# Two more seven-product pairs in three branch blocks, sums by accumulating transfers, and four plain pairs in front of the first

## The chip, the cores and the metric

The kernel runs on one core of a Trainium2 chip. The metric is the time of one execution in microseconds of the device, lower is better. The time before is the median of three runs, 1035.17 us (1033.79 to 1035.41).

The engines named below: TensorE (PE in the profile, its weight loads PEld) multiplies; VectorE (DVE), ScalarE (ACT) and GpSimd (POOL) work on tensors; SyncE (SP) issues the weight loads from memory. Each engine takes its instructions from one queue, in order.

## The reference

One decoder layer on 256 tokens of width 2048, with two branches that are merged and projected once more:

```python
h = _rmsnorm(x, pre_norm_g)
proj = einsum('bsd,de->bse', h, w_in)      # q_a, c_kv, k_rope, z_mla, c_in, ..., g_mla, g_conv
...                                        # latent attention; a gated short convolution
y_mla  = einsum('bse,ed->bsd', attn, w_o_mla)
y_conv = einsum('bse,ed->bsd', b_gate * conv * silu(z_conv), w_o_conv)
merged = sigmoid(g_mla) * y_mla + sigmoid(g_conv) * y_conv
out = einsum('bsd,de->bse', merged, w_out)
return x + _rmsnorm(out, post_norm_g)
```

Everything is float32. The change touches four products of 256 x 2048 by 2048 x 2048: `g_mla` and `g_conv` (columns of `w_in`), `y_mla` and `y_conv`.

## The kernel before

*Weights.* They are streamed in units of 1 MB, in the order of a list `plan`, in which a unit's number is its place. SyncE loads a unit into a `raw` tile (three of them); ScalarE rounds it into a high part `whi`, VectorE subtracts to get a low part `wlo` (`split_act`, line 282 and 283). Both are in halves of 128x1024 (`whi122_0`, `whi122_1024`), five slots each: a half can be written when the half five places before it was read for the last time. A product is three matmuls, high by high, high by low, low by high (`product`), each 128x128 by 128x512.

*Blocks.* The four products at issue are cut in eight blocks (n, c): n = 0 and 1 are the two gates, n = 2 and 3 the two branches (`y_mla`, `y_conv`), c is the half of the columns, 1024 wide. A block has eight pairs, one unit each, so block (0,0) has the units 113 to 120, (0,1) 121 to 128, and so on to (3,1), 169 to 176. A *plain pair* has 8 products of 2x2 quarters (two row tiles of x, two column halves, two inner halves), 24 matmuls. A *seven-product pair* is the same 2x2 product by Strassen's way in Winograd's form: 7 products, 21 matmuls. It needs sums of weight quarters, which VectorE makes (`ts`, `split_seven`, line 224) and which are split in high and low too (`th`, `tl`, two slots each), and sums of activation quarters (`mixed`, lines 1008 and 1012, split into `mix0`, `mix3`, `mix5`, kept for later blocks). Which pairs have seven products is in `fast`: pairs 0, 3 and 5 (`FAST`) in the gates' blocks, but 0 and 3 in (0,0); none in the branches' blocks.

*A fast block* (`fast_block`) accumulates its products in eight PSUM banks, p1, q5, q7, q6, p2, q3, q4, d22. Plain pairs go to p2, q3, q4 and d22 alone. Behind the last seven-product pair p1, q5, q6 and q7 are complete, and `first_sums` adds them up (one copy on ScalarE, line 1053, and four sums on VectorE, line 1050); it is put in the program at the start of the pair after the last fast one. `last_sums` adds p2, q3, q4 and d22 behind the block's end, again on VectorE. The bank of p1, that of q5 and so on are the same ones in the next block, whose pair 0 begins with p1, q5, q7, q6. Then ScalarE makes the sigmoid of the gates (line 1115).

*A plain block* (`plain_block`) accumulates in four banks. Behind it VectorE multiplies the sums by the gates (lines 1131, 1137), and in the blocks of n = 3 adds the branches.

*The order of the work.* TensorE's matmuls are kept in program order; the instructions of the other engines are put in order by a scheduler, within what their data allow, so each engine's queue is fixed before the run. `pair_order` sets the order of pairs, and so of units. Between pairs, `between(i)` puts other work into the program: the mixed activations and the turning of the attention's and convolution's results.

Of the kernel before, what the change touches and what calls it, by code (L numbers as in the profile page):

```python
# [84 lines left out]
def tile_layer(ctx: ExitStack, tc: tile.TileContext, xw, w0, xb, x, pos, pvec, post_g, wc, wz, wcv, wkr, wqk, wqr, wv, cwr, wd, wo, out):  # L85
# [53 lines left out]
            u_head[i][j] = add(wcv[i, j])  # L139

    pair_order = {(n, c): list(range(PAIRS)) for n in range(4) for c in range(2)}
    pair_order[0, 0] = [1, 2, 4, 0, 6, 3, 5, 7]
    fast = {(n, c): FAST if n < 2 else () for n in range(4) for c in range(2)}
    fast[0, 0] = FAST[:2]
    u_d, seven = {}, set()
    for n in range(4):
        for c in range(2):
# [148 lines left out]
    def col(name, k=0):  # L296
        o, _ = PV[name]
        return pv[:, o + k : o + k + 1]

    const.tile([P, P], F32, name="place")  # L300
    mhalf = const.tile([P, 1], F32, name="mhalf")
    nc.gpsimd.memset(mhalf[:, :], -0.5)
    hpi = const.tile([P, 1], F32, name="hpi")
# [4 lines left out]
    one = nc.const_aps.tensor(1.0, [P, P], F32)  # L308
    for _ in range(8):
        matmul(idle[:, :P], one, one, start=True, stop=True)  # L310
    const.tile([P, LINE - 8 + 112 + P], F32, name="const_pad")
    cos_t = const.tile([P, S], F32, name="cos_t")
    sin_t = const.tile([P, S], F32, name="sin_t")
    r_x = const.tile([P, S], F32, name="r_x")
    r_both = const.tile([P, LINE], F32, name="r_both")
    nc.gpsimd.memset(r_both[:, :], 0.0)
    r_col, r_sq = r_both[:, :NT], r_both[:, NT : 2 * NT]
# [92 lines left out]
    def input_norm():  # L410
        ss = squares("x", [(x_tok[:, t, :], x_tok[:, t, :]) for t in range(NT)])
        v = temp("v_x", (P, NT), tag="rms_v")
        nc.vector.tensor_scalar(v[:, :], ss[:, :], 1.0 / D, EPS, op0=ALU.mult, op1=ALU.add)
        inverse_root(r_col[:, :], v[:, :])
        nc.vector.tensor_tensor(r_sq[:, :], r_col[:, :], r_col[:, :], op=ALU.mult)

        rt = temp("r_turned", (P, LINE), bufs=1)
        temp("pad_n", (P, S - LINE), bufs=1)
        nc.vector.transpose(rt[:, :], r_both[:, :])
        far = dram.tile([NT, S // NT], F32, name="far_r")  # L420
        rows_of = rt[:, :].rearrange("(q y) x -> y q x", q=4)
        for t in range(NT):
            tc.keep_in_program_order(
                nc.gpsimd.dma_start(out=far[t, :].rearrange("(q x) -> q x", q=4), in_=rows_of[t])
            )
        return lambda: tc.keep_in_program_order(
            nc.gpsimd.dma_start(out=r_x[:, :], in_=far[:, :].rearrange("t s -> (t s)").unsqueeze(0).to_broadcast([P, S]))
        )


# [4 lines left out]
        nc.vector.tensor_tensor(dst, ps[:, :S], t[:, :], op=ALU.add)  # L435

    def rows(dst):
        tc.keep_in_program_order(nc.vector.tensor_tensor(dst, dst, r_x[:, :], op=ALU.mult))


    tables_pi = temp("ta_i", (P, SQ), I32, 1)
# [1 line left out]
    def tables():  # L443
# [38 lines left out]
        for o in range(4):  # L482
# [3 lines left out]
                    tc.keep_in_program_order(nc.gpsimd.tensor_copy(dst[to, SQ * q : SQ * (q + 1)], src[ti, :]))  # L486
        yield
        tc.keep_in_program_order(
            nc.vector.tensor_scalar(sin_t[:, :], sin_t[:, :], col("sign"), None, op0=ALU.mult)
        )  # L490
        yield

    def rope(src, dst, keep=False):

        a, b = temp("rp_a", bufs=1), temp("rp_b", bufs=1)
        first = nc.vector.tensor_tensor(a[:, :], src, cos_t[:, :], op=ALU.mult)
        if keep:
            tc.keep_in_program_order(first)
        for q in range(4):
            i, o = slice(32 * q, 32 * q + 32), slice(32 * (q ^ 1), 32 * (q ^ 1) + 32)  # L500
            nc.vector.tensor_tensor(b[o, :], src[i, :], sin_t[i, :], op=ALU.mult)
        nc.vector.tensor_tensor(dst, a[:, :], b[:, :], op=ALU.add)
# [453 lines left out]
    def ring(tag, dt, size=HALF, bufs=2):  # L956
        return lambda name: sp.tile([P, size], dt, name=name, tag=tag, bufs=bufs)

    sums, sums_hi, evens, sums_lo = (
        ring(tag, dt, size) for tag, dt, size in (("ts", F32, HALF), ("th", F32R, HALF), ("ev", F32, R), ("tl", F32R, HALF))  # L960
    )
    for r in (sums, sums_hi, evens):
        r("home")
    gate = [[None] * NT for _ in range(2)]

    def gate_tile(n, t):
# [34 lines left out]
        for t in range(NT):  # L1001
            split_turned(src[:, c, t, :], place, c, t)

    def mixed(k):
        tmp = evens(f"xr{k}")
        f = tmp[:, :].rearrange("p (j s) -> p j s", j=2)
        ks = slice(2 * k, 2 * k + 2)
        nc.vector.tensor_tensor(f, x_both[:, ks, :S].bitcast(F32), x_both[:, ks, S:].bitcast(F32), op=ALU.add)
        raw = evens(f"xm{k}")
        a11, a21, a12, a22 = (f[:, j, t * P : (t + 1) * P] for j in range(2) for t in range(2))  # L1010
        m7, m5, m6, m3 = (raw[:, j * P : (j + 1) * P] for j in range(4))
        minus = lambda o, a, b: nc.vector.tensor_tensor(o, a, b, op=ALU.subtract)
        minus(m7, a21, a11)
        minus(m5, a21, a22)
        minus(m6, a11, m5)
        minus(m3, a12, m6)
        split_act(mix[k][:, 0, :], mix[k][:, 1, :], raw[:, :])

    def mix_part(k, j):
        return tuple(mix[k][:, o, j * P : (j + 1) * P] for o in range(2))  # L1020
# [4 lines left out]
    def fast_block(n, c, part, outs, between):  # L1025
# [19 lines left out]
        for at, (k, name, a, b) in enumerate(calls):  # L1045
            firsts.setdefault(name, at)
            lasts[name] = at
        t_a, t_b = (evens(f"ev{i}_{n}{c}")[:, :] for i in range(2))
        (o11, o12), (o21, o22) = outs
        tt = lambda o, a, b, op=ALU.add: nc.vector.tensor_tensor(o, a, b, op=op)  # L1050

        def first_sums():
            nc.scalar.activation(t_a, q["p1"][:, :], AF.Copy)
            tt(t_b, q["q6"][:, :], t_a, ALU.subtract)
            tt(o12, q["q5"][:, :], t_b)
            tt(o21, q["q7"][:, :], t_b)
            tt(o22, q["q5"][:, :], o21)

        def last_sums():
            tt(o11, q["p2"][:, :], t_a)  # L1060
            tt(o12, q["q3"][:, :], o12)
            tt(o21, q["q4"][:, :], o21, ALU.subtract)
            tt(o22, q["d22"][:, :], o22)

        at = 0
        for i, k in enumerate(order):
# [8 lines left out]
        last_sums()  # L1075

    def plain_block(n, c, part, between):
        tags = ("mm",) * 4 if c else ("st", "o", "cv", "cv")
        q = {
            (t, j): bank(f"sq{n}{c}_{t}{j}", tag=tag, bufs={"mm": 4, "cv": 2}.get(tag, 1))  # L1080
            for (t, j), tag in zip(((0, 0), (0, 1), (1, 0), (1, 1)), tags)
        }
        order = pair_order[n, c]
        for at, k in enumerate(order):
            w = take(u_d[n, c, k])
            between(at)
            for (t, j), ps in q.items():
                for i in range(2):
                    b = w({(0, 0): 0, (1, 1): 1, (1, 0): 2, (0, 1): 3}[i, j], R)
                    product(ps[:, :], part(2 * k + i, t), b, at == i == 0, at == PAIRS - 1 and i == 1)  # L1090
        return q
# [3 lines left out]
            split_turned(gate[0][t][:, c * R : (c + 1) * R], m_place, c, t)  # L1095

    make_identity(nc, ident[:, :])
    for n in range(2):
        if n:
            lstack.close()  # L1100
            last_gate = spool.enter_context(tc.tile_pool(name="last_gate", bufs=1))
            gate[1][1] = last_gate.tile([P, D], F32, name="g1_1")
        for c in range(2):

            def between(i):
                if n == c == 0 and i in (1, 3, 5):
                    mixed(FAST[i // 2])
                if n == c == 1 and i in (2, 4, 6):
                    split_group(at_place, at_t, i // 2 - 1)

            outs = [[gate[n][t][:, columns(c, j)] for j in range(2)] for t in range(NT)]
            fast_block(n, c, x_part, outs, between)
            for t in range(NT):
                for o in outs[t]:
                    nc.scalar.activation(o, o, AF.Sigmoid, scale=r_col[:, t : t + 1])
    def between(c, i):
        if (c, i) == (0, 1):
            split_group(at_place, at_t, 3)
        elif (c, i) == (0, 3):
            astack.close()  # L1120
            cv_first["area"] = cv_stack.enter_context(tc.tile_pool(name="cv_first", bufs=1, side="right")).tile(
                [P, KD // 2, 2 * S], F32R, name="cv_first"
            )
        if (c, i) in ((0, 4), (0, 6), (1, 3), (1, 5)):
            split_group(cv_place, cv_t, {(0, 4): 0, (0, 6): 1, (1, 3): 2, (1, 5): 3}[c, i])

    for c in range(2):
        q = plain_block(2, c, x_part, lambda i: between(c, i))
        for (t, j), ps in q.items():
            g = gate[0][t][:, columns(c, j)]  # L1130
            nc.vector.tensor_tensor(g, ps[:, :], g, op=ALU.mult)
    for c in range(2):
        q = plain_block(3, c, cv_part, lambda i: features(i - 4) if c and i in (4, 5) else None)
        steps = []
        for (t, j), ps in q.items():
            m, y = (gate[i][t][:, columns(c, j)] for i in range(2))
            nc.vector.tensor_tensor(y, ps[:, :], y, op=ALU.mult)
            nc.vector.tensor_tensor(m, m, y, op=ALU.add)  # L1138
            steps.append((turned(m, y, 4), m))
            steps[-1][0][0]()  # L1140
        for (_, come), m in steps:
            come(m)

    def out_product(ps, t, w, kk):
        for k4 in range(4):
# [4 lines left out]
        for t in range(NT):  # L1150
            out_product(pss[t], t, w, kk)

    pss = [[bank(f"out0_{t}", tag=tag, bufs=1) for t, tag in enumerate(("st", "o"))]]
    pss += [[bank(f"out1_{t}", tag="cv", bufs=2) for t in range(NT)], [bank(f"out2_{t}") for t in range(NT)]]
    for i, (c, kk) in enumerate(out_order[:6]):
        w = take(u_out[c, kk])
        if i == 5:
# [189 lines left out]
```

## Time and profile before

| | us |
|---|---|
| median of 3 runs | 1035.17 |
| lowest, highest | 1033.79, 1035.41 |
| the profiled execution's own time | 1034.48 |
| its span in the profile | 1032.7 |
| TensorE busy | 1022.6 |
| VectorE busy | 747.4 |
| ScalarE busy | 543.9 |
| GpSimd busy | 179.0 |

The mean granted clock of TensorE is 0.997 of full speed. The profile is of one execution; its times are microseconds from the start of the span. In rows of instructions, tiles have the program's names without numbers, `out<-in`; "xN" counts the instructions in a row. A row with an engine's idle time says in brackets what ended it.

### The profile page before, as it was taken

How to read it: one execution, taken by the hardware profiler on the slowest of the kernel's cores; microseconds unless marked ns; L12 is line 12 of the kernel's file. 1: busy time of each engine (PE TensorE's matmuls, PEld its weight loads, DVE VectorE, ACT ScalarE, POOL GpSimd, SP SyncE). 2: the span in 40 equal slices, each digit the busy share in tenths (PEclk: the TensorE clock that was granted, in tenths of full speed). 3: DMA queues.
4: the chain of work that ended last, by engine and by line, in shares of the span. 5: the costliest groups of instructions: out<-in, count | busy, mean ns of one | idle time of the engine just before them, and what ended most of it. 6: DMA issues, size and time to landing. Idle time of an engine off the chain costs nothing.

```text
span 1032.7 us, 12827 instructions
## 1 busy us (share of the span) xinstructions
PE 1022.6 (99%) x4651; PEld 851.5 (82%) x4651; DVE 747.4 (72%) x1062; ACT 543.9 (53%) x764; POOL 179.0 (17%) x344
## 2 busy tenths in 40 slices
PE   9999999999999999999999989999999999999998
PEld 7888888888888888888888868888888888888886
DVE  7588777787777777777877798898875554756572
ACT  7665545655456454564555546555654443344451
POOL 4540421104301223112133120000000000214000
PEclk9999999999999999999999989999999999999999
DMA  9775866568665676757676755555555555577852
GB/s 357 276 260 202 279 205 234 213 201 282 218 246 197 220 263 211 273 192 244 229 269 222 260 183 178 226 206 204 204 198 182 193 202 196 197 258 246 344 184 81
DMA packets 44528, 233.26 MB, mean 226 GB/s; under 512 B 7953, under 2 KB 10513, under 8 KB 21553
## 3 DMA queue, kind: packets, MB, share of 16 engines
q1 hardware_dynamic: 32400, 199.67, 54.8%
q0 software_dynamic: 11632, 29.48, 8.8%
q10 hardware_dynamic: 432, 3.29, 0.8%
q8 instruction: 36, 0.59, 0.2%
q14 instruction: 28, 0.22, 0.1%
HBM read 215.66 MB, written 12.58 MB: 221 GB/s over the span
## 4 chain that ended last, share of the span: by engine, by line
PE 97%; DVE 2%; DMA 0%; ACT 0%; issue 0%
PE cv L90 34%; PE sq L90 17%; PE q L90 8%; PE z L90 8%; PE out L90 8%; PE p L90 4%; PE d L90 2%; PE kn L90 2%; PE qa L90 2%; PE qn L90 2%; PE vv L90 2%; PE ckv L90 2%; PE sc L90 1%; PE qr L90 1%; PE o L90 1%; DVE wlo L283 1%
## 5 line engine op out<-in xcount | busy, mean ns | idle before, releaser
L283 DVE TENSOR_TENSOR wlo<-raw,whi 128x1024 fp32r<-128x1024 f32 (+1 forms) x370 | 431.8, 1179 | 202.8 <-ACT whi L282 195.4
L282 ACT ACTIVATE whi<-raw 128x1024 fp32r<-128x1024 f32 (+1 forms) x372 | 373.2, 1021 | 376.0 <-PE cv L90 116.9
L90 PE MATMUL cv<-whi,x_both 128*128 128x512 f32 x1024 | 319.8, 389 | 0.0
L90 PEld LDWEIGHTS cv<-whi,x_both 128*128 128x128 f32 x1024 | 192.3, 188 | 39.4
L90 PE MATMUL cv<-wlo,x_both 128*128 128x512 f32 x512 | 199.6, 390 | 0.0
L90 PE MATMUL sq<-whi,x_both 128*128 128x512 f32 x384 | 118.8, 389 | 0.0
L90 PEld LDWEIGHTS cv<-wlo,x_both 128*128 128x128 f32 x512 | 96.1, 188 | 19.5 <-DVE wlo L283 0.2
L90 PEld LDWEIGHTS sq<-whi,x_both 128*128 128x128 f32 x384 | 72.1, 188 | 15.0
L90 PE MATMUL z<-whi,x_both 128*128 128x512 f32 x256 | 80.0, 389 | 0.0
L90 PE MATMUL out<-whi,x_both 128*128 128x512 f32 x256 | 79.0, 389 | 0.0
L90 PE MATMUL sq<-wlo,x_both 128*128 128x512 f32 x192 | 74.7, 389 | 0.0
L367 POOL DMA_DIRECT2D far<-g x32 | 17.4, 551 | 322.5 <-DVE g L1138 289.9
L367 POOL DMA_DIRECT2D far<-via x64 | 35.2, 556 | 179.2 <-DVE via L359 178.9
L90 PEld LDWEIGHTS out<-whi,x_both 128*128 128x128 f32 x256 | 48.1, 188 | 9.9
L90 PEld LDWEIGHTS z<-whi,x_both 128*128 128x128 f32 x256 | 48.1, 188 | 9.9
L90 PE MATMUL q<-whi,x_both 128*128 128x512 f32 x168 | 55.1, 389 | 0.0
L90 PE MATMUL z<-wlo,x_both 128*128 128x512 f32 x128 | 49.8, 389 | 0.0
L90 PE MATMUL out<-wlo,x_both 128*128 128x512 f32 x128 | 49.8, 389 | 0.0
L90 PE MATMUL p<-whi,x_both 128*128 128x512 f32 x128 | 46.6, 391 | 0.0
L90 PEld LDWEIGHTS sq<-wlo,x_both 128*128 128x128 f32 x192 | 36.0, 188 | 7.4
L367 POOL DMA_DIRECT2D far<-cw x48 | 26.1, 551 | 79.1 <-DVE cw L359 79.1
L90 PE MATMUL sq<-whi,cv_first 128*128 128x512 f32 x128 | 39.7, 389 | 0.0
(253 smaller groups left out, 1433.0 us busy)
## 6 DMA issues: line engine op xcount, KB each, us to landing
raw<-wcv_dram SPq DMA_DIRECT2D x64, 1024.0 KB, 5.9
raw<-wd_dram SPq DMA_DIRECT2D x64, 1024.0 KB, 4.8
raw<-wz_dram SPq DMA_DIRECT2D x16, 1024.0 KB, 4.8
raw<-wo_dram SPq DMA_DIRECT2D x16, 1024.0 KB, 5.0
raw<-wqk_dram SPq DMA_DIRECT2D x8, 1024.0 KB, 6.1
cw<-cwr_dram POOLq DMA_DIRECT2D x24, 256.0 KB, 6.2
raw<-wc_dram SPq DMA_DIRECT2D x4, 1024.0 KB, 10.4
raw<-wv_dram SPq DMA_DIRECT2D x4, 1024.0 KB, 4.8
```

What stands on the lines that cost most here:

```text
L90: return tc.keep_in_program_order(nc.tensor.matmul(*a, **kw))
L282: a = nc.scalar.activation(hi, src, AF.Copy)
L283: b = nc.vector.tensor_tensor(lo, src, hi.bitcast(F32), op=ALU.subtract)
L367: tc.keep_in_program_order(queue.dma_start(out=f[i], in_=m))
```

## The change

*Which pairs.* Pairs 0 and 3 have seven products in (2,0), (2,1) and (3,0) too, so all blocks but (3,1) are fast blocks. Their mixed activations are made by four more calls of `mixed`, of the attention's result in (1,1) and (2,0), of the convolution's in (2,1) and (3,0).

*Order of pairs.* In (0,0) four plain pairs stand in front of the first fast one: pair 0 moves from fourth to fifth place, pair 3 from sixth to seventh. `first_sums` of this block stands now in the program at the eighth pair, before at the seventh.

*Sums.* The partial sums of a block stay in two tiles of 128x1024, `low` and `high`. `last_sums` is now four copies from PSUM to the result on ScalarE, and two accumulating transfers issued by GpSimd, which add `low` and `high` to it: 14 transfers of 512 KB. What reads the results (the sigmoid, the multiplication by the gates) is put off to the third pair of the next block (`later`). `high` serves as room for `mixed`, too.

*Banks and tiles.* The block (3,1) and the output product change PSUM banks; `low` lies where three tables of the attention lay; the space that GpSimd's transfers have for their descriptors is set to 8192 bytes.

```diff
-    pair_order[0, 0] = [1, 2, 4, 0, 6, 3, 5, 7]
-    fast = {(n, c): FAST if n < 2 else () for n in range(4) for c in range(2)}
-    fast[0, 0] = FAST[:2]
+    pair_order[0, 0] = [1, 2, 4, 6, 0, 5, 3, 7]
+    fast = {(n, c): FAST if n < 2 else FAST[:2] for n in range(4) for c in range(2)}
+    fast[0, 0], fast[3, 1] = FAST[:2], ()
...
+    low = const.tile([P, HALF], F32, name="low")
+    cos_t, sin_t, r_x = (low[:, i * S : (i + 1) * S] for i in range(3))
...
+    high = sp.tile([P, HALF], F32, name="high")
...
+        part0, part1, part2, part3 = (w[:, j * R : (j + 1) * R] for w in (low, high) for j in range(2))
+        tt = lambda o, name, b, op: nc.vector.tensor_tensor(o, q[name][:, :], b, op=op)
 
         def first_sums():
-            nc.scalar.activation(t_a, q["p1"][:, :], AF.Copy)
-            tt(t_b, q["q6"][:, :], t_a, ALU.subtract)
-            tt(o12, q["q5"][:, :], t_b)
-            tt(o21, q["q7"][:, :], t_b)
-            tt(o22, q["q5"][:, :], o21)
+            nc.scalar.activation(part0, q["p1"][:, :], AF.Copy)
+            tt(part3, "q6", part0, ALU.subtract)
+            tt(part1, "q5", part3, ALU.add)
+            tt(part2, "q7", part3, ALU.subtract)
+            tt(part3, "q5", part2, ALU.subtract)
 
         def last_sums():
-            tt(o11, q["p2"][:, :], t_a)
-            tt(o12, q["q3"][:, :], o12)
-            tt(o21, q["q4"][:, :], o21, ALU.subtract)
-            tt(o22, q["d22"][:, :], o22)
+            for t, (names, w) in enumerate(((("p2", "q3"), low), (("q4", "d22"), high))):
+                for j, name in enumerate(names):
+                    nc.scalar.activation(outs[t][:, j * R : (j + 1) * R], q[name][:, :], AF.Copy)
+                tc.keep_in_program_order(nc.gpsimd.dma_start(out=outs[t], in_=w[:, :], accum_op=ALU.add))
...
+    mixes_at = {
+        (0, 0, 1): (at_place, 0), (0, 0, 3): (at_place, 3), (0, 0, 5): (at_place, 5),
+        (1, 1, 5): (at_place, 0), (2, 0, 0): (at_place, 3),
+        (2, 1, 2): (cv_place, 0), (3, 0, 1): (cv_place, 3),
+    }
...
+        if i == 2:
+            while later:
+                later.pop(0)()
...
-    nc = bacc.Bacc("TRN2", target_bir_lowering=False, num_devices=1)
+    nc = bacc.Bacc("TRN2", target_bir_lowering=False, num_devices=1, dynamic_dma_scratch_size=8192)
```

The order of instructions at three places on VectorE. In names the last figure is a tile's number; `ts`, `th`, `tl` and `wlo` carry the unit's number first, q and p the block.

First, block (0,0), ahead of the low half of mix0, before (unit 116 is the first fast pair):

```order
L283 TENSOR_TENSOR wlo117_0_5715<-raw117_5665,whi117_0_5714 128x1024
L1012 TENSOR_TENSOR xm0_5634<-xr0_5632,xm0_5634 128x128
L283 TENSOR_TENSOR tl116_0_5675<-ts116_0_5671,th116_0_5673 128x1024
L224 TENSOR_TENSOR ts116_1_5672<-ts116_1_5672,raw116_5622 128x512
...
L224 TENSOR_TENSOR ts118_0_5758<-raw118_5712 128x1024
L283 TENSOR_TENSOR wlo117_1024_5719<-raw117_5665,whi117_1024_5718 128x1024
L1008 TENSOR_TENSOR xr3_5722<-x_both_104 128x512
L283 TENSOR_TENSOR wlo118_0_5756<-raw118_5712,whi118_0_5754 128x1024
L283 TENSOR_TENSOR tl116_1_5676<-ts116_1_5672,th116_1_5674 128x1024
L283 TENSOR_TENSOR mix0_5570<-xm0_5634,mix0_5570 128x512
```

And after (unit 117 is the first fast pair):

```order
L283 TENSOR_TENSOR wlo117_0_5696<-raw117_5658,whi117_0_5694 128x1024
L283 TENSOR_TENSOR tl117_0_5702<-ts117_0_5698,th117_0_5700 128x1024
L224 TENSOR_TENSOR ts117_1_5699<-ts117_1_5699,raw117_5658 128x512
...
L283 TENSOR_TENSOR wlo117_1_5697<-raw117_5658,whi117_1_5695 128x512
L283 TENSOR_TENSOR wlo118_0_5749<-raw118_5692,whi118_0_5748 128x1024
L1005 TENSOR_TENSOR high_5563<-x_both_101 128x512
L224 TENSOR_TENSOR ts119_0_5783<-raw119_5746 128x1024
L283 TENSOR_TENSOR tl117_1_5703<-ts117_1_5699,th117_1_5701 128x1024
L283 TENSOR_TENSOR mix0_5567<-high_5563,mix0_5567 128x512
```

The instruction for mix0 keeps its place beside the weights; the pair that needs it has moved one unit back.

Second, the end of block (0,0), with the four sums on VectorE of `first_sums`. Before:

```order
L1050 TENSOR_TENSOR ev1_00_5587<-q6_00_5585,ev0_00_5586 128x512
L283 TENSOR_TENSOR tl121_0_5888<-ts121_0_5884,th121_0_5886 128x1024
L283 TENSOR_TENSOR wlo120_1024_5846<-raw120_5799,whi120_1024_5845 128x1024
L1050 TENSOR_TENSOR g0_0_5572<-q5_00_5583,ev1_00_5587 128x512
L1050 TENSOR_TENSOR g0_1_5573<-q7_00_5584,ev1_00_5587 128x512
L283 TENSOR_TENSOR wlo121_0_5882<-raw121_5839,whi121_0_5880 128x1024
L283 TENSOR_TENSOR tl121_1_5889<-ts121_1_5885,th121_1_5887 128x1024
L1050 TENSOR_TENSOR g0_1_5573<-q5_00_5583,g0_1_5573 128x512
L283 TENSOR_TENSOR wlo121_1_5883<-raw121_5839,whi121_1_5881 128x512
L283 TENSOR_TENSOR wlo122_0_5946<-raw122_5878,whi122_0_5945 128x1024
```

After:

```order
L283 TENSOR_TENSOR wlo122_1024_5935<-raw122_5862,whi122_1024_5934 128x1024
L224 TENSOR_TENSOR ts124_0_5999<-raw124_5959 128x1024
L283 TENSOR_TENSOR mix5_5565<-high_5563,mix5_5565 128x512
L283 TENSOR_TENSOR wlo123_0_5962<-raw123_5928,whi123_0_5961 128x1024
L224 TENSOR_TENSOR ts124_1_6000<-ts124_0_5999,raw124_5959 128x512
L1045 TENSOR_TENSOR high_5563<-q6_00_5582,low_95 128x512
L224 TENSOR_TENSOR ts124_1_6000<-ts124_1_6000,raw124_5959 128x512
L1045 TENSOR_TENSOR low_95<-q5_00_5580,high_5563 128x512
L1045 TENSOR_TENSOR high_5563<-q7_00_5581,high_5563 128x512
L1045 TENSOR_TENSOR high_5563<-q5_00_5580,high_5563 128x512
```

The four sums have moved behind weights of the units 122 and 123, of which 122 is the next block's second; before, they stood among those of 120 and 121.

Third, block (3,0), around its pair 3 (unit 164). Before:

```order
L283 TENSOR_TENSOR wlo163_1024_7542<-raw163_7501,whi163_1024_7541 128x1024
L283 TENSOR_TENSOR wlo164_0_7572<-raw164_7535,whi164_0_7571 128x1024
L283 TENSOR_TENSOR wlo164_1024_7576<-raw164_7535,whi164_1024_7575 128x1024
L283 TENSOR_TENSOR wlo165_0_7606<-raw165_7569,whi165_0_7605 128x1024
L283 TENSOR_TENSOR wlo165_1024_7610<-raw165_7569,whi165_1024_7609 128x1024
L283 TENSOR_TENSOR wlo166_0_7640<-raw166_7603,whi166_0_7639 128x1024
```

After:

```order
L283 TENSOR_TENSOR wlo164_0_7666<-raw164_7621,whi164_0_7664 128x1024
L1008 TENSOR_TENSOR high_5563<-high_5563 128x128 x2
L283 TENSOR_TENSOR tl164_1_7673<-ts164_1_7669,th164_1_7671 128x1024
L283 TENSOR_TENSOR wlo164_1_7667<-raw164_7621,whi164_1_7665 128x512
L283 TENSOR_TENSOR wlo165_0_7716<-raw165_7662,whi165_0_7715 128x1024
...
L283 TENSOR_TENSOR wlo165_1024_7720<-raw165_7662,whi165_1024_7719 128x1024
L283 TENSOR_TENSOR wlo166_0_7747<-raw166_7713,whi166_0_7746 128x1024
L283 TENSOR_TENSOR mix3_5566<-high_5563,mix3_5566 128x512
L1045 TENSOR_TENSOR high_5563<-q6_30_7589,low_95 128x512
```

A plain pair's two halves have become a seven-product pair's sums, and the mixed activation that this pair reads stands behind halves of the units 165 and 166.

More of the change, by code (lines that the diff above doesn't have):

```diff
@@ L426, in input_norm @@
         return lambda: tc.keep_in_program_order(
-            nc.gpsimd.dma_start(out=r_x[:, :], in_=far[:, :].rearrange("t s -> (t s)").unsqueeze(0).to_broadcast([P, S]))
+            nc.gpsimd.dma_start(out=r_x, in_=far[:, :].rearrange("t s -> (t s)").unsqueeze(0).to_broadcast([P, S]))
         )
@@ L495, in rope @@
         a, b = temp("rp_a", bufs=1), temp("rp_b", bufs=1)
-        first = nc.vector.tensor_tensor(a[:, :], src, cos_t[:, :], op=ALU.mult)
+        first = nc.vector.tensor_tensor(a[:, :], src, cos_t, op=ALU.mult)
         if keep:
@@ L957, in ring @@
         return lambda name: sp.tile([P, size], dt, name=name, tag=tag, bufs=bufs)
[L959 to L962, printed above, removed]
+    sums, sums_hi, sums_lo = (ring(tag, dt) for tag, dt in (("ts", F32), ("th", F32R), ("tl", F32R)))
+    for r in (sums, sums_hi):
         r("home")
+    high = sp.tile([P, HALF], F32, name="high")
     gate = [[None] * NT for _ in range(2)]
@@ L1002, in split_group, with mixed @@
             split_turned(src[:, c, t, :], place, c, t)
[L1004 to L1009, printed above, removed]
+    def mixed(place, k):
+        area, o = place(2 * k)
+        f, raw = high[:, :R].rearrange("p (j s) -> p j s", j=2), high[:, R:]
+        ks = slice(o, o + 2)
+        nc.vector.tensor_tensor(f, area[:, ks, :S].bitcast(F32), area[:, ks, S:].bitcast(F32), op=ALU.add)
         a11, a21, a12, a22 = (f[:, j, t * P : (t + 1) * P] for j in range(2) for t in range(2))
@@ L1016, in mixed @@
         minus(m3, a12, m6)
-        split_act(mix[k][:, 0, :], mix[k][:, 1, :], raw[:, :])
+        split_act(mix[k][:, 0, :], mix[k][:, 1, :], raw)
     def mix_part(k, j):
@@ L1097, in tile_layer, with between @@
     make_identity(nc, ident[:, :])
[L1098 to L1119, printed above, removed]
+    splits_at = {
+        (1, 1, 2): (at_place, at_t, 0), (1, 1, 4): (at_place, at_t, 1), (1, 1, 6): (at_place, at_t, 2), (2, 0, 1): (at_place, at_t, 3),
+        (2, 0, 4): (cv_place, cv_t, 0), (2, 0, 6): (cv_place, cv_t, 1), (2, 1, 3): (cv_place, cv_t, 2), (2, 1, 5): (cv_place, cv_t, 3),
+    }
[3 more added lines that the diff above has]
+        (2, 1, 2): (cv_place, 0), (3, 0, 1): (cv_place, 3),
+    }
+    features_at = {(3, 1, 5): 0, (3, 1, 6): 1}
+    later = []
+    def between(n, c, i):
+        if (n, c, i) in splits_at:
+            split_group(*splits_at[n, c, i])
+        if (n, c, i) in mixes_at:
+            mixed(*mixes_at[n, c, i])
+        if (n, c, i) == (2, 0, 3):
             astack.close()
@@ L1123, in between @@
             )
[L1124 to L1133, printed above, removed]
-        steps = []
[L1135 to L1140, printed above, removed]
+        if i == 2:
+            while later:
+                later.pop(0)()
@@ new lines, in between, with gated @@
+        if (n, c, i) in features_at:
+            features(features_at[n, c, i])
+    def gated(n, c, ys):
+        steps = []
+        for t in range(NT):
+            for j in range(2):
+                y, (m, g) = ys[t][j], (gate[i][t][:, columns(c, j)] for i in range(2))
+                if n == 2:
+                    nc.vector.tensor_tensor(m, y, m, op=ALU.mult)
+                    continue
+                nc.vector.tensor_tensor(g, y, g, op=ALU.mult)
+                nc.vector.tensor_tensor(m, m, g, op=ALU.add)
+                steps.append((turned(m, g, 4), m))
+                steps[-1][0][0]()
@@ L1141, in tile_layer, with opened @@
         for (_, come), m in steps:
             come(m)
+    def opened(n, c, outs):
+        for t in range(NT):
+            nc.scalar.activation(outs[t], outs[t], AF.Sigmoid, scale=r_col[:, t : t + 1])
+    for n in range(4):
+        if n == 1:
+            lstack.close()
+            last_gate = spool.enter_context(tc.tile_pool(name="last_gate", bufs=1))
+            gate[1][1] = last_gate.tile([P, D], F32, name="g1_1")
+            branch = [last_gate.tile([P, HALF], F32, name=f"y{t}") for t in range(NT)]
+        for c in range(2):
+            pick, step = cv_part if n == 3 else x_part, lambda i: between(n, c, i)
+            if not fast[n, c]:
+                q = plain_block(n, c, pick, step)
+                gated(n, c, [[q[t, j][:, :] for j in range(2)] for t in range(NT)])
+                continue
+            if n < 2:
+                outs = [gate[n][t][:, c * HALF : (c + 1) * HALF] for t in range(NT)]
+            else:
+                outs = [y[:, :] for y in branch]
+            fast_block(n, c, pick, outs, step)
+            if n < 2:
+                later.append(lambda a=(n, c, outs): opened(*a))
+            else:
+                later.append(lambda a=(n, c, [[o[:, j * R : (j + 1) * R] for j in range(2)] for o in outs]): gated(*a))
@@ L1151, in out_products @@
             out_product(pss[t], t, w, kk)
-    pss = [[bank(f"out0_{t}", tag=tag, bufs=1) for t, tag in enumerate(("st", "o"))]]
-    pss += [[bank(f"out1_{t}", tag="cv", bufs=2) for t in range(NT)], [bank(f"out2_{t}") for t in range(NT)]]
+    pss = [[bank(f"out{c}_{t}") for t in range(NT)] for c in range(2)]
+    pss.append([bank(f"out2_{t}", tag=tag, bufs=1) for t, tag in enumerate(("st", "o"))])
     for i, (c, kk) in enumerate(out_order[:6]):
```

17 lines of the change are left out of this document (5 added, 12 removed).

## The prediction

> **What bounds the kernel now.** I read the engines' busy times first, then the chain of work that ended last, then TensorE's timeline where that chain stops being TensorE's.
>
> ```profile
> PE 1022.6 (99%) x4651; PEld 851.5 (82%) x4651; DVE 747.4 (72%) x1062; ACT 543.9 (53%) x764; POOL 179.0 (17%) x344
> PE 97%; DVE 2%; DMA 0%; ACT 0%; issue 0%
> 612.31 3.35 PE q L90 x7
> 763.60 174.08 PE sq L90 x768
> 937.68 87.05 PE out L90 x384
> ```
>
> The first row gives busy us, the second shares of the chain, the others pieces of the chain (start, length, instructions). TensorE bounds the kernel. The fourth row is the pace: 174.08/768 = 0.22667 us for a matmul, so 5.44 us for a plain pair (24 matmuls) and 4.76 for one with seven products (21). From 763.60 to the end of the products nothing but TensorE is on the chain: the four branch blocks run at full pace today. Only one place in the blocks waits, at 612, in block (0,0):
>
> ```profile
> 590.23 0.39 PE L90 MATMUL p<-whi,x_both 128*128 128x512 f32 x1
> 607.04 0.39 PE L90 MATMUL p<-whi,x_both 128*128 128x512 f32 x1
> 609.74 0.77 PE L90 MATMUL q<-th,mix 128*128 128x512 f32 x1 [2.31 <-issue]
> 612.31 1.22 PE L90 MATMUL q<-th,mix 128*128 128x512 f32 x2 [1.38 <-DVE mix L283]
> 616.32 0.39 PE L90 MATMUL p<-whi,x_both 128*128 128x512 f32 x1
> 617.92 0.39 PE L90 MATMUL p<-whi,x_both 128*128 128x512 f32 x1
> 639.00 0.39 PE L90 MATMUL p<-whi,x_both 128*128 128x512 f32 x1
> 599.83 0.66 DVE L1008 TENSOR_TENSOR xr<-x_both 128x512 f32<-128x512 f32 x1
> 611.56 0.69 DVE L283 TENSOR_TENSOR mix<-xm,mix 128x512 fp32r<-128x512 f32 x1
> 590.00:635.00 45.00, 41.31 (x173) 33.25 (x172) 42.87 (x62) 22.94 (x27) 5.50 (x10) 0.92 0.53 187
> 763.60:807.00 43.40, 43.40 (x193) 35.93 (x193) 25.08 (x26) 20.38 (x25) 0.00 (x0) 1.00 0.55 194
> ```
>
> Rows begin with start and duration; brackets give the idle time and what ended it. The last two are stretches: length, then busy us (and instructions) of PE, PEld, DVE, ACT, POOL, then granted clock. Block (0,0) starts at 590.23. Three plain pairs and the three p1 products bring TensorE to 607.27, where the first mixed activation is wanted; VectorE, busy 42.87 of 45.00 us, finishes it at 611.56 + 0.69 = 612.25. The 18 matmuls due from 607.27 on are through at 617.92: 10.65 us for 18 x 0.22667 = 4.08, so 6.57 lost. Of it 1.97 is the slower clock (the 9 matmuls from 612.31 to 616.32 took 4.01 us for 2.04); the rest is waiting.
>
> **The change, part by part.** *Fewer matmuls.* Six more pairs with seven products, three matmuls less in each: 18 x 0.22667 = **-4.1 us**. TensorE is the bound at that place, so this counts in full.
>
> *Four plain pairs in front.* TensorE reaches the first fast pair at 590.23 + 4 x 5.44 = 611.99 and wants the low half of mix0 in that pair's sixth matmul, at 613.1. VectorE's rows from the `high<-x_both` of pair 0 to that instruction, added by the durations below, come to 12.4 us in the new order and 12.4 in the old (599.83 to 612.25). So it is ready at about 612.3, 0.8 early. The second fast pair now begins at 622.2; its mix3 has in front of it the work of one more pair, and I find it ready within 0.4 us of need. **-6.6 us**, and **+0.3** for those two margins (0 to 2).
>
> *The same sums, one pair later in the block.* This is the term that decides. first_sums now comes with one pair left in the block, not two, and its last operation frees the bank in which the next block's q5 is made; that q5 comes right after the next block's three p1 matmuls. Before, with VectorE's and ScalarE's prices:
>
> ```profile
> 609.29 1.23 DVE L283 TENSOR_TENSOR wlo<-raw,whi 128x1024 fp32r<-128x1024 f32 x1
> 610.42 1.23 DVE L283 TENSOR_TENSOR tl<-ts,th 128x1024 fp32r<-128x1024 f32 x1
> 612.16 0.69 DVE L224 TENSOR_TENSOR ts<-ts,raw 128x512 f32<-128x512 f32 x1
> 612.76 0.50 DVE L1012 TENSOR_TENSOR xm<-xr 128x128 f32<-128x128 f32 x2
> 630.82 1.28 DVE L1050 TENSOR_TENSOR g<-q,ev 128x512 f32<-128x512 f32 x2
> 634.29 0.69 DVE L1050 TENSOR_TENSOR g<-q,g 128x512 f32<-128x512 f32 x1
> 639.20 0.69 DVE L1050 TENSOR_TENSOR g<-d,g 128x512 f32<-128x512 f32 x1 [0.67 <-PE d L90]
> 622.88 2.01 ACT L282 ACTIVATE whi<-raw 128x1024 fp32r<-128x1024 f32 x2 [2.15 <-PE d L90]
> 624.79 0.58 ACT L1053 ACTIVATE ev<-p 128x512 f32<-128x512 f32 x1
> ```
>
> Start to start, VectorE takes 1.13 us for 128x1024, 0.60 for 128x512 and 0.20 for 128x128; ScalarE 0.96 and 0.58. The first_sums end at 634.29 + 0.69 = 634.98, 4.7 us before the q5 of the next block (639.00 + 0.68 = 639.68). That margin goes. In the new order (the rows are with the change) the last of them stands on VectorE's queue behind `wlo122_1024`, which reads `whi122_1024`, which ScalarE can write only when its slot is free. The slot was `whi120_1024`'s, and the fourth matmul from the block's end is its last reader; let T be the time at which the next block's first matmul is due (590.23 + 186 x 0.22667 = 632.4). That reader begins at T - 0.91 and lasts 0.39, so it is done at T - 0.52, as the 622.88 row shows ScalarE waiting for a `d` product in the same way. Then: ScalarE's 1.04 to T + 0.52; on VectorE wlo122_1024 1.13, ts124_0 1.13, mix5 0.60, wlo123_0 1.13, ts124_1 0.60, high<-q6 0.60, ts124_1 0.60, low<-q5 0.60, high<-q7 0.60, high<-q5 0.69: 7.68, to T + 8.2. TensorE wants the bank at T + 0.68. So it waits **+7.5 us** (bounds: 0 if these rows could be passed, which a queue in order excludes unless ScalarE comes earlier; 8.6 if one more 128x1024 row is left over in front). After that wait the clock is slow, as after the one at 607: **+2.0**, from the 1.97 above.
>
> *Two more pairs with seven products in the blocks (2,0), (2,1) and (3,0).* A plain pair costs VectorE two 1.13 (2.26), a seven-product pair 1.13 + 2 x 0.60 for its sums, 1.13 + 0.60 for wlo and 2 x 1.13 for tl: 6.3, so 8.1 more in a block, and mixed (0.60 + 4 x 0.20 + 0.60 = 2.0) and first_sums (2.4) on top: 12.5. On the 25.08 of the row from 763.60 that is 37.6 in about 42: covered on the whole, but not in its order. In (2,0) mix3 stands behind wlo149_1024, in the same trap of a slot free at T - 0.52: ScalarE to T + 0.52, wlo 1.13, mix3 0.69: T + 2.3, wanted in the pair's sixth matmul, T + 1.13: **+1.2**. In (3,0) it stands behind wlo165_1024 and wlo166_0: T + 0.52 + 1.13 + 1.13 + 0.69 = T + 3.5: **+2.4**. In (2,1) mix0 and mix3 exist already. Bounds for the two together: 0 (if VectorE's rows there run before the slot comes free) and 3.6 + 2 x 2.0 of slow clock. I take 3.6 without slow clock, since the wait is in two parts (for the high half, then for the low half), each shorter than the 2.31 us in the 609.74 row.
>
> The Trainium skill's page "TensorE: Matmul & The Clock Gate" (Part 1: The HAM clock gate) has the clock halved only after an idle window of about 3.4 us, by which (3,0) pays no slow clock. The row disagrees: a wait of 2.31 us was followed by a matmul of 0.77. By that row a whole wait of 2.4 us would cost 2.0 more, and the sum would be 1040.4.
>
> *The accumulating transfers.* 14 of 512 KB, from SBUF to SBUF, issued by GpSimd (idle in these blocks: 0.00 in the row from 763.60). The trace has no such transfer. The nearest, with KB and median us from issue to landing:
>
> ```profile
> mv<-cv_f POOLq DMA_DIRECT2D x8, 254.0 KB, 4.4
> mv<-cv_f POOLq DMA_DIRECT2D x8, 252.0 KB, 5.4
> cv_f<-far POOLq DMA_DIRECT2D x8, 256.0 KB, 6.6
> raw<-wc_dram SPq DMA_DIRECT2D x4, 1024.0 KB, 10.4
> ```
>
> The first two are SBUF to SBUF like the new ones, at half the bytes; so 6 us, with 4.4 and 10.4 as ends. What waits for them stands in queues in order: ScalarE's sigmoid and VectorE's gating. The tightest is (2,1) (and its like in (3,0) and (3,1)): the second transfer is issued after the copy of d22, at about T + 1.1; behind it on VectorE stand `high<-cv_first` 0.60, a gating product 0.60 and wlo155_1024 1.22, whose first use by TensorE is four matmuls into the third pair, T + 4.76 + 5.44 + 0.9 = T + 11.1. So 7.6 us from issue to landing are hidden. At 6 us the cost is nothing, plus **+0.5** for landings above the median; if a transfer takes 10.4, it is 2.8 us at three places and 2.0 of slow clock at each: +14.
>
> The Trainium skill's page "DMA: Bandwidth & Descriptors" (Anatomy of one DMA, SWDGE path) gives 2.0 us plus bytes/436e3, an estimate of 3.2 us for 512 KB and of 2.6 for 254 KB; the row has 4.4 for the latter, so I go by the row. With 3.2 the 0.5 would go from the sum.
>
> *The rest.* In all blocks four sums on VectorE (2.4 us) become four copies on ScalarE (2.3); ScalarE has 23 us free in the row from 763.60, and the next block's p2 bank is wanted only after 12 matmuls (2.7 us): nothing. Block (3,1), the output products and the tail keep their matmuls, on banks that are free at least as early: nothing.
>
> **Sum**, against the profiled execution's 1034.48 us: -4.1 - 6.6 + 0.3 + 7.5 + 2.0 + 1.2 + 2.4 + 0.5 = +3.2, so 1037.7. The median of the runs is 0.69 above that execution, hence **1038.4**.
>
> **Rivals.**
> *The other side: the first_sums come in time.* They would if ScalarE could write whi122_1024 before the block's last matmuls, so that VectorE is through by T + 0.68; the point is 7.5 us earlier. Then 1034.48 - 4.1 - 6.6 + 0.3 + 1.2 + 2.4 + 0.5 = 1028.2, and 1028.9 as a median. For it: VectorE made these sums 4.7 us early before. Against it: the slot rule above, and no row of the trace shows ScalarE ahead of such a slot.
> *Slow transfers.* Above 7.6 us each, sigmoid and gating hold up the weights behind them: 1038.4 + 14 = 1052 at 10.4 us. For it: they read, add and write, beside weight loads that keep the DMA engines busy at 0.55 (the row from 763.60). Against: every row of 256 KB is under 7.
> *The branch blocks hide their mixes.* Without the 3.6 the time is 1034.8, within the bound of no change. For it: VectorE has 18 us free in such a block. Against: the order of its queue, which has the work of the next pair in front.
>
> **How the numbers follow.** This kernel's runs tell about 0.2% from no change, 2.1 us: faster is under 1033.1, slower above 1037.2. Forecast (1036 to 1042): 0.57, of which a fifth lies below 1037.2. Other side: 0.12. Slow transfers: 0.18. Hidden mixes: 0.13. So faster 0.12; same 0.13 + 0.11 = 0.24; slower 0.64. The range runs from 1033.5 (leaving out the other side) to 1047 (about half of the slow transfers); the forecast's own is 1036 to 1042.
>
> **What the changed profile would show.** No wait before the first fast pair's q5 near 612; a wait of 7 to 8 us before the first `q<-th,mix` of (0,1), near 633, ended by VectorE's `high<-q,high`, with a slow clock behind it; waits of 1 to 2.5 us for mix in (2,0) and (3,0); the transfers landing in 5 to 7 us; 18 matmuls fewer. A wait near 633 under 2 us would break the sum at its main term; a chain with pieces of DMA in (2,1) to (3,1) would speak for slow transfers.

## The result, and the profile after

The changed kernel takes 1050.38 us (median of four runs, 1048.19 to 1052.3), the kernel before in the same session 1034.48 (1033.61 to 1035.41): a ratio of 1.0153, 95% interval 1.0128 to 1.0178. It is 16 us slower, where 4 were forecast. The profiled execution is the longest of the four, 1052.3 us. The first rows of the page, busy us by engine and shares of the chain of work that ended last:

```profile
PE 1026.5 (98%) x4633; PEld 851.2 (81%) x4633; DVE 776.4 (74%) x1112; ACT 571.3 (54%) x803; POOL 192.4 (18%) x358
PE 17%; DVE 4%; issue 3%; DMA 2%; ACT 0%; POOL 0%; POOLq 0%; DVEq 0%
```

The 18 matmuls are gone (x4651 became x4633). TensorE has 4.1 us less of work and yet 3.9 us more of busy time, since more of its matmuls ran on a slow clock (the granted clock is 0.988 on the mean, before 0.997). The chain is no longer TensorE's throughout. It is followed back only to 771.63, so the shares come to about a quarter of the span, and it begins there with a transfer. TensorE's timeline (start, duration, in brackets the idle time ahead and what ended it) at the places where it waits:

```profile
632.63 0.39 PE L90 MATMUL p<-whi,x_both 128*128 128x512 f32 x1
640.81 0.77 PE L90 MATMUL q<-th,mix 128*128 128x512 f32 x1 [7.80 <-DVE high L1045]
645.98 0.39 PE L90 MATMUL q<-whi,mix 128*128 128x512 f32 x1
738.80 0.50 PE L90 MATMUL p<-wlo,x_both 128*128 128x512 f32 x1 [1.91 <-DVE wlo L283]
786.37 0.39 PE L90 MATMUL p<-whi,x_both 128*128 128x512 f32 x1
790.24 0.79 PE L90 MATMUL q<-th,mix 128*128 128x512 f32 x1 [3.48 <-ACT mix L282]
796.12 0.39 PE L90 MATMUL q<-wlo,mix 128*128 128x512 f32 x1
879.04 0.50 PE L90 MATMUL q<-th,mix 128*128 128x512 f32 x1 [1.35 <-ACT mix L282]
880.48 0.73 PE L90 MATMUL q<-th,mix 128*128 128x512 f32 x2 [0.71 <-DVE mix L283]
921.80 0.50 PE L90 MATMUL sq<-wlo,cv_first 128*128 128x512 f32 x1 [2.22 <-DVE wlo L283]
```

The wait near 612 is gone, and the forecast one stands at the start of (0,1): from 632.63 to 645.98 are 13.35 us for 13 matmuls that need 2.95, so 10.4 lost, 7.8 of it waiting, the rest slow clock. After that come four places more. Counted in the same way (time between starts of matmuls beyond 0.2267 us each), in the profiled executions of the kernel before, of this one and of two that are told of below (1034.48, 1052.3, 1041.96 and 1034.89 us):

| us lost | before | changed | plain copies | no transfers |
|---|---|---|---|---|
| (0,0), first fast pair | 6.6 | 0.2 | 0.2 | 0.2 |
| start of (0,1) | 0 | 10.4 | 10.1 | 10.8 |
| (1,1), third, fifth and seventh pair | 0 | 3.1 | 0 | 0 |
| (2,0), mix3 | 0 | 6.6 | 2.8 | 0 |
| (3,0), mix3 | 0 | 4.2 | 4.2 | 0 |
| (3,1), third pair | 0 | 4.1 | 0 | 0 |
| sum | 6.6 | 28.6 | 17.3 | 11.0 |

The sum explains the span: 28.6 - 6.6 - 4.1 = 17.9, and the spans differ by 1050.5 - 1032.7 = 17.8.

The transfers, by group (KB, median us from issue to landing):

```profile
g<-low POOLq DMA_DIRECT2D x4, 512.0 KB, 5.1
g<-high POOLq DMA_DIRECT2D x4, 512.0 KB, 11.0
y<-low POOLq DMA_DIRECT2D x3, 512.0 KB, 4.6
y<-high POOLq DMA_DIRECT2D x3, 512.0 KB, 5.1
```

Two of them as pieces of the chain (start, length):

```profile
771.63 11.23 DMA g<-high
908.99 8.51 DMA y<-high
```

VectorE's timeline, three rows that wait:

```profile
732.91 1.22 DVE L224 TENSOR_TENSOR ts<-raw 128x1024 f32<-128x1024 f32 x1 [5.43 <-DMA raw<-wd_dram]
782.88 0.69 DVE L1005 TENSOR_TENSOR high<-x_both 128x512 f32<-128x512 f32 x1 [0.29 <-DMA g<-high]
917.53 1.29 DVE L1129 TENSOR_TENSOR g<-y,g 128x512 f32<-128x512 f32 x2 [4.15 <-DMA y<-high]
```

And the stretch around the transfer behind (1,1): length, busy us of PE, PEld, DVE, ACT, POOL, granted clock, busy share of the DMA engines, GB/s:

```profile
770.00:786.00 16.00, 16.00 (x72) 13.23 (x72) 12.57 (x16) 10.50 (x13) 0.86 (x1) 1.00 0.94 264
```

Ten of the 14 land in 4.5 to 6.4 us, near the 6 that were estimated. Three of the four out of `high` behind the gates' blocks take 10.9 to 11.2, and the one behind (3,0) takes 8.5. In the stretch above, around the third, the DMA engines are busy at 0.94 (0.55 in the block (2,0) before). Each late landing then reaches TensorE by another road: in (2,0) the mixed activation cannot write `high` until 782.86, in (3,1) the gating stands on VectorE's queue ahead of the weights until 917.5, and in (1,1) a weight load is late itself (732.91, a load of 7.7 us where most take 4.8).

### The profile page after: what moved, and what is told of

The parts are those of the page before. It is cut to its first block, busy times and chain, and to the rows that moved or that the text cites. A ratio compares the mean times of both kernels' runs of the same rounds, so it can differ in the third digit from the quotient of the medians.

```text
span 1050.5 us, 12902 instructions
## 1 busy us (share of the span) xinstructions
PE 1026.5 (98%) x4633; PEld 851.2 (81%) x4633; DVE 776.4 (74%) x1112; ACT 571.3 (54%) x803; POOL 192.4 (18%) x358
## 5 line engine op out<-in xcount | busy, mean ns | idle before, releaser
L90 PE MATMUL q<-whi,x_both 128*128 128x512 f32 x296 | 97.2, 389 | 0.0
L90 PE MATMUL p<-whi,x_both 128*128 128x512 f32 x208 | 75.8, 393 | 0.0
L90 PEld LDWEIGHTS q<-whi,x_both 128*128 128x128 f32 x296 | 55.5, 188 | 11.7
L90 PE MATMUL q<-wlo,x_both 128*128 128x512 f32 x148 | 57.6, 389 | 0.0
L90 PE MATMUL d<-whi,x_both 128*128 128x512 f32 x148 | 51.6, 389 | 0.0
L90 PE MATMUL q<-th,mix 128*128 128x512 f32 x102 | 38.3, 431 | 13.3 <-DVE high L1045 7.8
L283 DVE TENSOR_TENSOR tl<-ts,th 128x1024 fp32r<-128x1024 f32 x34 | 41.4, 1217 | 12.4 <-ACT th L282 12.4
L90 PEld LDWEIGHTS p<-whi,x_both 128*128 128x128 f32 x208 | 39.6, 190 | 8.3
L282 ACT ACTIVATE th<-ts 128x1024 fp32r<-128x1024 f32 x34 | 35.8, 1054 | 17.7 <-DVE ts L224 12.8
## 6 DMA issues: line engine op xcount, KB each, us to landing
raw<-wc_dram SPq DMA_DIRECT2D x4, 1024.0 KB, 10.1
```

What stands on the lines that cost most here:

```text
L90: return tc.keep_in_program_order(nc.tensor.matmul(*a, **kw))
L282: a = nc.scalar.activation(hi, src, AF.Copy)
L283: b = nc.vector.tensor_tensor(lo, src, hi.bitcast(F32), op=ALU.subtract)
```

## The experiments

Beside each kernel ran the kernel before, at 1033.9 to 1034.9 us.

**1. The old order of pairs in the changed kernel.**

```diff
-    pair_order[0, 0] = [1, 2, 4, 6, 0, 5, 3, 7]
+    pair_order[0, 0] = [1, 2, 4, 0, 6, 3, 5, 7]
```

> The changed kernel with the pairs of the first block in the order of before (first_sums two pairs before the block's end). Theory: the new order itself costs 10.4 us (7.95 of waiting before the first q5 of the second block, 2.4 of slow clock) and saves the 6.6 of the old wait near 612, so undoing it gives 1050.4 - 10.4 + 6.6 = 1046.6 us. Rival: the order is a gain as it was drawn up, and the transfers and branch blocks cost everything: then undoing it makes the kernel slower, 1057 us.

It took 1050.90 us (1048.34 to 1051.45): the wait at the start of (0,1) went and the one near 612 came back, 7.0 us, as expected. But 4.4 us were lost at a new place, the start of (1,0):

```profile
692.43 0.50 PE L90 MATMUL p<-whi,x_both 128*128 128x512 f32 x1 [0.69 <-ACT whi L282]
694.49 0.50 PE L90 MATMUL p<-wlo,x_both 128*128 128x512 f32 x1 [1.55 <-DVE wlo L283]
```

Ahead of that, the sigmoid on ScalarE's queue, with the weights behind it, waits for a transfer out of `low`:

```profile
689.34 1.15 ACT L1138 ACTIVATE g<-g,r_both 128x1024 f32<-128x1024 f32 x1 [6.62 <-DMA g<-low]
```

And the landing times of all transfers into or out of `low` in this kernel:

```profile
DMA to landing us min/median/max: 4.5/5.1/10.2
```

One, the one waited for here, takes 10.2 us, where none took over 6.4 in the changed kernel. The time, 1046.6 in the theory, thus came out 4.3 above it. About four microseconds of shift at the start go with another transfer being slow, so the order's cost can't be had by undoing it alone.

**2. The new order of pairs in the kernel before.** The same edit the other way round.

> The kernel before with only the new order of pairs in the first block. Theory: the wait of about 7.9 us before the first q5 of the second block forms here too, since the four sums on VectorE stand behind wlo122_1024 in the same way: 1034.5 - 6.6 + 10.4 = 1038.3 us. Rival: without the transfers and the shared tile the sums come earlier and only the old wait goes: 1027.9 us.

1039.65 us (1038.76 to 1040.34; ratio 1.0053, 1.0038 to 1.0068). The wait forms without any transfer, 9.8 us lost, with 1.8 more just ahead of it, where p1's bank is not yet copied out:

```profile
634.93 0.50 PE L90 MATMUL p<-whi,x_both 128*128 128x512 f32 x1 [1.53 <-ACT ev L1053]
642.85 0.80 PE L90 MATMUL q<-th,mix 128*128 128x512 f32 x1 [6.95 <-DVE g L1050]
```

So the four plain pairs in front cost by themselves more than they save, because the sums come one pair later.

**3. Plain copies in the place of accumulating transfers.** The results are then the partial sums.

```diff
-                tc.keep_in_program_order(nc.gpsimd.dma_start(out=outs[t], in_=w[:, :], accum_op=ALU.add))
+                tc.keep_in_program_order(nc.gpsimd.dma_start(out=outs[t], in_=w[:, :]))
```

> The changed kernel with plain transfers in the place of the accumulating ones, same tiles, same bytes (the result then has the partial sums in the place of the full sums). Theory of contention: what makes the transfer of high take 11 us behind the gates' blocks is that two weight loads of 1 MB run in the same microseconds; a plain copy takes 10 to 11 us there too, and the kernel stays within 2 us of 1050.4. Rival, the read, add and write of the accumulation: plain copies land in 4.5 to 6.5 us everywhere, the weight loads beside them in about 5, and the kernel comes to 1037 to 1040 us.

1038.83 us (1038.17 to 1041.96): 11.5 us of the 16 go with the accumulation alone. The landing times of the three transfers out of `high` from 680 to 790 us and, in the same stretch, of the weight loads, first of the changed kernel, then with plain copies:

```profile
DMA to landing us min/median/max: 10.9/11.1/11.2
DMA to landing us min/median/max: 4.7/4.8/10.6
```

```profile
DMA to landing us min/median/max: 6.5/6.7/9.6
DMA to landing us min/median/max: 4.6/4.8/8.9
```

And two groups of the same kernel that are slowed less (KB, median us):

```profile
g<-low POOLq DMA_DIRECT2D x4, 512.0 KB, 3.7
y<-high POOLq DMA_DIRECT2D x3, 512.0 KB, 3.4
```

Neither theory had it alone: a plain copy is faster but is slowed too (9.6 at worst), and so is a weight load beside it (8.9).

**4. No transfers.** The same line left out; `low` and `high` are not added to the result.

> The changed kernel without the 14 transfers (the partial sums in low and high are not added to the result). Both theories: the waits in (1,1), (2,0) and (3,1) behind a late transfer go, 2.2 + 0.9 + 6.3 + 4.4 = 13.8 us less, of which the mixed activation in (2,0) takes back about 1.2: 1037.8 us. The wait of 7.9 us in the second block and that of 2 to 4 us in (3,0) stay. If the time stays above 1045 us, the transfers are not the cause.

1034.11 us (1032.94 to 1034.89), 3.7 better than expected. The waits in (1,1) and (3,1) go as expected, but those for mix3 in (2,0) and (3,0) go as well, in full. The two more seven-product pairs in a branch block cost nothing then; in that kernel's order mix3 stands further ahead on VectorE's queue, by 7 rows in (2,0) and by 21 in (3,0), since `high` has no transfer to wait for.

**5. The sums on VectorE, as before.** The 18 matmuls and the new order kept.

```diff
+        t_a, t_b = (low[:, j * R : (j + 1) * R] for j in range(2))
+        (o11, o12), (o21, o22) = ((o[:, :R], o[:, R:]) for o in outs)
...
         def last_sums():
-            for t, (names, w) in enumerate(((("p2", "q3"), low), (("q4", "d22"), high))):
-                ...
+            tt(o11, "p2", t_a, ALU.add)
+            tt(o12, "q3", o12, ALU.add)
+            tt(o21, "q4", o21, ALU.add)
+            tt(o22, "d22", o22, ALU.add)
```

> The changed kernel with its sums on VectorE as before (no transfers, no copies by ScalarE), the 18 matmuls less and the new order of pairs kept. Theory: everything that the change lost in the branch blocks and in (1,1) comes from the transfers, and the mixed activations stand ahead of the weights again; in the first block the last of the four sums stands just ahead of wlo122_1024 here, so the wait there is under 2 us: 1034.3 - 4.1 - 6.6 + 2 = 1025.6 us. Rival: eight more microseconds of VectorE in each branch block and the order of pairs are what costs; then waits for mix of 1 to 4 us stay in (2,0) and (3,0) and it comes to 1031 us or more.

1029.02 us (1028.67 to 1030.0), ratio 0.9955 (0.9943 to 0.9968): faster than before, though 3.4 above the theory's number. No mixed activation is late. What is left is 2.2 and 1.1 us at the start of (0,1) and 2.0 in (2,0), where the sums of the weights of the second fast pair (`th`, `tl`) come late; the rows at the start of (0,1), and one of those in (2,0):

```profile
635.03 0.47 PE L90 MATMUL q<-th,mix 128*128 128x512 f32 x1 [1.92 <-DVE g L1046]
639.54 0.50 PE L90 MATMUL q<-th,x_both 128*128 128x512 f32 x1 [0.85 <-DVE g L1046]
779.83 0.50 PE L90 MATMUL q<-tl,mix 128*128 128x512 f32 x1 [1.14 <-DVE tl L283]
```

With the last of the four sums ahead of `wlo122_1024` in the queue, the wait at that place is 1.9 us in the place of 7.8.

**6. Four plain pairs in front and two pairs behind, in the kernel before.**

```diff
-    pair_order[0, 0] = [1, 2, 4, 0, 6, 3, 5, 7]
+    pair_order[0, 0] = [1, 2, 4, 6, 0, 3, 5, 7]
```

> The kernel before with the order 1, 2, 4, 6, 0, 3, 5, 7 in the first block: four plain pairs in front, and two pairs again behind the last fast one. Theory: the old wait near 612 goes (6.6 us) and first_sums come in time: 1028 us, or up to 1030 if mix3, which is wanted at 617.9 now, is late. Rival: four pairs in front are too many or VectorE is late anyway, and a wait of 4 us or more stays: 1032 us or more.

1034.87 us (ratio 1.0010, 1.0001 to 1.0019): the theory's 1028 failed. The wait near 612 goes and one for mix3 comes at the second fast pair, now right behind the first; 7.1 us are lost there:

```profile
619.79 0.80 PE L90 MATMUL q<-th,mix 128*128 128x512 f32 x1 [2.61 <-ACT mix L282]
```

In the changed kernel a plain pair stands between the two seven-product pairs, and there 0.2 us are lost.

**7. Another tile for the mixed activation of (2,0).**

```diff
+    def mixed(place, k, room=None):
+        room = high if room is None else room
...
+            mixed(*mixes_at[n, c, i], branch[1] if (n, c, i) == (2, 0, 0) else None)
```

> The changed kernel; only mix3 for (2,0) is made in the tile y1, which is free there, in the place of high. Theory: the 6.6 us lost in (2,0) are the wait of that mixed activation until the transfer out of high has landed; without it at most 1 us is lost there and the kernel comes to 1050.4 - 6 = 1044.5 us. Rival: VectorE's queue in (2,0) is late by itself (1.2 us and slow clock by my sum) or late weight loads hold it: 1048 us or more.

1043.26 us (1042.82 to 1044.2): 7.1 less than the changed kernel. In (2,0) 1.0 us is lost in the place of 6.6:

```profile
771.97 0.50 PE L90 MATMUL q<-th,mix 128*128 128x512 f32 x1 [0.70 <-DVE high L1046]
```

So 5.6 of the 6.6 was the wait of the mixed activation for its tile. Most of the rest of the gain is in (3,0), where mix3 is still made in `high`: there the loss falls from 4.2 to 1.5, with mix3 one 128x1024 row of weights further ahead in the queue.

**8. No weight loads beside the transfers.** The second to fourth pair of (1,0), (1,1) and (2,0) take the weights of the pair before.

```diff
+    small = [u_d[n, c, 0] + k for n, c in ((1, 0), (1, 1), (2, 0)) for k in (1, 2, 3)]
...
+        if i in small:
+            raws[i] = raws[i - 1]
+            return
```

> The changed kernel without the weight loads of the second to fourth pair of (1,0), (1,1) and (2,0), which are the ones in flight beside the transfers behind (0,1), (1,0) and (1,1) (those pairs use the weights of the pair before, so the result is another). Theory that it is both, accumulation and shared engines: without loads beside it the transfer of high lands in 5 to 6 us in these places, as it did in (0,0) and in the branch blocks, in place of 11. Rival, that the accumulation or the order of these two transfers alone makes it slow there: 9 us or more.

The same two rows as in experiment 3, of this kernel:

```profile
DMA to landing us min/median/max: 4.4/4.4/5.4
DMA to landing us min/median/max: 4.7/4.8/5.0
```

The three transfers that took 10.9 to 11.2 us take 4.4 to 5.4, accumulating as before, while the one behind (3,0), whose loads are left in, takes 8.5 as in the changed kernel. (One run, 1037.94 us; the time says little, since loads are left out.) With experiment 3: for 11 us it takes both, the accumulation and loads in the same microseconds.

**9. One seven-product pair in the first block, sums on VectorE.**

```diff
-    pair_order[0, 0] = [1, 2, 4, 6, 0, 5, 3, 7]
+    pair_order[0, 0] = [1, 2, 4, 6, 0, 3, 5, 7]
-    fast[0, 0], fast[3, 1] = FAST[:2], ()
+    fast[0, 0], fast[3, 1] = FAST[:1], ()
...
```

The sums are changed as in experiment 5.

> The kernel with sums on VectorE (d_order_new) with a single seven-product pair in the first block, at its fifth place, so that first_sums come three pairs before the block's end. Theory: the 3.3 us that d_order_new still loses around the start of the second block (2.2 and 1.1) are the late first_sums; they go, three matmuls more cost 0.7: 1029.0 - 3.3 + 0.7 = 1026.4 us. Rival: the wait at the block's start is VectorE's backlog whatever stands in it, and 1029 us or more stays.

1026.19 us (1025.83 to 1026.6), ratio 0.9914 (0.9901 to 0.9928): 0.2 from the theory, and the fastest of all. TensorE loses 2.0 us in the blocks, all in (2,0), and the chain is TensorE's again:

```profile
PE 98%; DMA 0%; ACT 0%; DVE 0%; issue 0%
```

## Why the prediction was wrong

*Right.* The 18 matmuls, -4.1. The old wait, -6.6, and 0.3 for the margins (0.2 measured). The main term, the four sums one pair late: 7.5 + 2.0 forecast, 7.8 of waiting and 10.4 in all measured, ended by `high<-q,high` as named; and its queue, row by row:

```profile
632.84 1.23 DVE L283 TENSOR_TENSOR wlo<-raw,whi 128x1024 fp32r<-128x1024 f32 x1 [1.64 <-ACT whi L282]
639.26 1.41 DVE L1045 TENSOR_TENSOR high<-q,high 128x512 f32<-128x512 f32 x2
```

The first is `wlo122_1024`, which starts when ScalarE has its slot. The block began at T = 632.17, so it starts at T + 0.67, where I had T + 0.52; the last sum ends at 640.67, T + 8.5, where I had T + 8.2.

*Wrong: the term of the accumulating transfers.* I took 6 us for each and 0.5 in all. Without a weight load in flight they take 4.4 to 5.8, so the estimate from the nearest rows was good for a transfer by itself. The step that failed is "At 6 us the cost is nothing": it priced the transfer by a row of its own kind and not by what runs beside it. Behind three of the gates' blocks weight loads are issued in the same microsecond, and the transfer out of `high` took about 11. The sum also had no term for the loads that a transfer slows; a late load stands behind the 3.1 us lost in (1,1). I had put "they read, add and write, beside weight loads" among the reasons for the rival, with 0.18, and its 1052 us is near what came, but by luck, through other places: the tightest was not (2,1), where the transfers took 5, but (2,0), where I had looked only at weights and not at `mixed`, which writes into the tile that the transfer reads.

*Wrong: 1.2 and 2.4 for mix3 as a cost of the seven-product pairs.* The size for (3,0) was near (2.4 forecast; 1.35 and 0.71 of waiting, 4.2 with the slow clock that I left out), and so was the way, mix3 in the queue behind weights. What put it there was not the pairs: experiments 4 and 5 have the same pairs and no wait for mix3 (5 loses 2.0 in (2,0) to the sums of the weights). mix3 stood behind the weights of units 165 and 166 because its tile was shared with a transfer. In (2,0), where 1.2 was forecast, 6.6 was lost, and there mix3 waited for the transfer itself. So both belonged to the transfers, whose cost, with the order of the queues that they bring, is 1050.4 - 1034.1 = 16.3 us, not 0.5.

*The clock.* I set the waits in (3,0) at no slow clock because each part was shorter than the 2.31 us in the old row. A wait of 1.35 us with one of 0.71 behind it was followed by matmuls at the slow spacing (0.43 us) until 884.6: 2.1 us.

What stays open: why some transfers are slowed and others beside a load are not. In the changed kernel each of the four transfers that took over 8 us has a load issued within 0.6 us of it, before or after. Behind (2,0) and (2,1) the load is issued 1.3 and 1.5 us after the transfer out of `high`: the load is slowed, to 7.0 and 6.1 us, and the transfer takes 5.1 and 5.0. But in experiment 7 a transfer took 8.7 us with loads issued 2.2 us before and 2.4 us after it, so this is a pattern and no rule. A shift of a few microseconds moves it (experiment 1), and nothing here tells how to place a transfer safely.

## What to carry to other kernels

A transfer that replaces work on an idle-enough engine has a price beside the traffic that it will meet, not the price of its kind alone; look at what the weight stream does in the same microseconds, and at the slowest landing, not the median. Where a buffer is shared between such a transfer and another step, that step is late as often as the transfer is, and the scheduler can move it back even when the transfer is quick (4.2 us in (3,0) behind a plain copy that landed in 2.8). With the sums left on VectorE the same pairs gave 1029.0 us, and one seven-product pair fewer 1026.2.

## What the runs showed of the hardware

An accumulating transfer of 512 KB between two places in SBUF took 4.4 to 5.8 us with no weight load in flight (behind (0,0) and, in experiment 8, behind the gates' other blocks), a plain one 2.8 and 2.9 (behind (0,0) in experiment 3). Where 1 MB weight loads were issued in the same microsecond, the accumulating one out of `high` took 8.5 to 11.2, and those loads took as much as 10.6 in the place of 4.8; the plain one took 6.5 to 9.6 behind the gates' blocks and 3.5 behind (3,0). The cost is thus paid twice, by the transfer and by the loads that it meets.
